# A bidirectional delta-rule scan: four of eight operators evicted by two engines, and the order of the stage and of the end laid out anew

## The chip, the cores and the metric

The kernel runs on one core of a Trainium2 chip. The metric is the device time of one launch, in microseconds; lower is better. PE (TensorE) multiplies and PEld loads its weights; DVE (VectorE), ACT (ScalarE) and POOL (GpSimd) are the element-wise engines; SP (SyncE) issues DMAs. Each engine runs its instructions in one fixed order, and an instruction at the front of its queue that waits holds everything behind it on that engine.

## The reference

One layer of a sequence model on 128 context tokens and 2048 latent tokens of width 1024, in float32:

```python
h    = rmsnorm(x, norm_g) * (1 + scale) + shift
r, k, v, g_a, b_gate, c_gate, u_conv, g_b = split(h @ w_in)
r, k, v = token_shift(r, k, v)
# head group A, 8 heads x 64, in two directions: the delta rule
def step(S, inp):
    r_t, w_t, k_t, v_t, kk_t, a_t = inp
    s_kk = einsum('bdhij,bdhj->bdhi', S, kk_t)
    S = (S * w_t[..., None, :] - s_kk[..., :, None] * (kk_t * a_t)[..., None, :]
         + v_t[..., :, None] * k_t[..., None, :])
    return S, einsum('bdhij,bdhj->bdhi', S, r_t)
ya = (groupnorm(sum of both directions) + bonus) * silu(g_a)
# head group B: a gated convolution of three taps
yb = b_gate * conv3(c_gate * u_conv) * silu(g_b)
out = rmsnorm(x + gate * (concat(ya, yb) @ w_out), final_g)
```

The outputs are the context and latent tokens and the final states S of the context.

## The kernel before

The launch has three parts. **Part 1** makes the modulation, the norm, the input projection (each float32 factor as a high and a low fp32r part, three products), the token shift, the gates and the convolution; it writes the scan's operands to DRAM. Its first products for the scan are begun early. **Part 2** is the scan, and **part 3** the output projection with its residual and last norm.

*The scan.* It is chunked: 64 tokens of a head pair are a unit. A stage is 8 units of one head pair in one direction and 8 in the other (its two groups, gi 0 and 1). There are 16 latent stages and one for the context (stage 15; the last one, 16, is latent), 17 in all. Within a unit the delta rule becomes matrix products, and between units a state of 64x64 per head is carried. A stage is written in words; the last digit is the group, and a digit ahead of it numbers halves or units:

- Gm, Qm, Fm: products of the operands on PE (L1019, L1028). Ge, Fe: their masks on DVE (L1037). Fa, Qe: copies on ACT (L1051, L1048).
- dg, ab, zi, pre: the diagonal blocks, turned and prepared (DVE L1058, L1063, L1081, L1082, ACT L1073 to L1075). I: the inverse of 32x32 triangles for both groups, 45 instructions on POOL in 15 steps of one L1091 and two L1094, each from the step before it.
- zr, zd (DVE L1102, L1105), c0, c1 (ACT L1111), U, bu, W, n (PE L1119, ACT L1122, PE L1127, ACT L1130): the inverse of the 64x64 triangles from those of the 32x32 ones. gh: operand copies on ACT (L1160, L1161).
- X, Xc: the solve on PE (L1171) and its eviction on ACT (L1175).
- E: eight operators a stage (16 matmuls each, L1189) into a PSUM tile of 128x512. Ev: the mask that evicts such a tile, on DVE (L1194), all 512 columns; of each 128 columns the first 64 meet ones in the mask.
- S, sv: one step of the state on PE (L1220: an operator times state and values, state and outputs at once) and the scaling of the new state on DVE (L1246). y: the outputs of four units, copied by ACT (L1267) or added by DVE (L1265). POOL clears the first state of the context (L1215) and copies a held state (L1213).
- fw, fr, fq, fm, T, fy, fa: the group norm and gate of a finished block of 512 tokens (L1298 to L1323), written to DRAM in mixT.

*What sets the order.* `SEQ` lists the words of one body; `word+d` does the word for the stage d later, so body b has the states of stage b, the operators of b and b+1, the inversion of b+2 and the products of b+3. Bodies 0 to 12 are this list again and again; from there on `LATE` lists every word with its stage (`word@stage`), and the words of part 3 among them. The orders of PE, DVE and ACT are those of the lists. POOL and SP are not under the lists; the framework places their instructions by what they depend on.

*PSUM.* Three pools lie beside each other: four buffers for the states and T, U, W, two "s" buffers, and two "m" buffers. `IN_PM` names the products that take "m"; the others, and E from stage 14 and X from stage 15 on, take "s".

*Words of part 3.* R closes the "m" pool and opens part 3. CL, CH, CD and WL, WH, WD load w_out's convolution and attention rows and split them in two (load L1468, high on ACT, low on DVE or POOL). AL, AH, AD and aL, aH, aD do that for the tokens of a tile (L1483, L1490). AP and AE are the convolution products of tiles 5, 6 and 7, done ahead, and their eviction (L1503 to L1505). P, B: convolution and attention products; Z, G, Q, ss, rt, rc, fo: gate, residual (POOL L1568) and norm.

Of the kernel before, what the change touches and what calls it, by code (L numbers as in the profile page):

```python
# [10 lines left out]
ALU = mybir.AluOpType  # L11
# [746 lines left out]
fsL0+1 gsL0+2 sv01 fr Ev100 Gm1+3 Ge1+3 dg1+3 W+1 S11 Qm1+3 gh11+1 gh00+1 ab+3 fq Fm0+3 S30 n+1 Qe1+3 Qm0+3  # L758
L0+4 sv11 Fa0+3 Qe0+3 zi+3 sv30 S40 Fe0+3 fm S21 sv40 sv21 Fm1+3 L1+4 X0+1 S50 pre+3 T sv50 Fa1+3 Fe1+3 S31
S60 sv31 Xc00+1 init+1 y00 Xc10+1 X1+1 S41 Xc01+1 sv60 S70 svL0+2 zr+2 sv41 E000+1 sv70 fy Xc11+1 Ev000+1  # L760
zd+2 S51 gh01+2 U+2 y01 Gm0+4 E001+1 c0+2
"""
IN_PM = "E001 E011 E101 E110 Fm1 Gm1 Qm0 Qm1 X1".split()
IN_S = "T U W".split()
FIXED = 13
LATE = """
I@15 sv51@12 fa@10.1 Ge0@16 E110@13 Ev001@13 gh10@14 E010@13 Ev110@13 E100@13 gh00@14 Ev010@13 Gm1@16
fsL0@14 Ev100@13 gh11@14 S00@13 Ge1@16 S61@12 E111@13 c1@14 sv00@13 E011@13 sv61@12 bu@14 dg0@16 S10@13
Ev011@13 S71@12 E101@13 svL1@14 fw@11.0 sv10@13 sv71@12 y10@12 S20@13 fsL1@14 Ev111@13 S01@13 y11@12 W@14
sv20@13 sv01@13 Ev101@13 S30@13 n@14 S11@13 sv30@13 sv11@13 S40@13 fr@11.0 X0@14 sv40@13 fq@11.0 dg1@16  # L770
X1@14 fm@11.0 Xc00@14 ab@16 S50@13 S21@13 Xc10@14 T@11.0 Xc01@14 E000@14 sv50@13 sv21@13 S60@13 Ev000@14
# [10 lines left out]
Ev000@15 fq@14.0 E011@15 fm@14.0 W@16 fsL1@16 gsL1@16 gh01@16 Ev001@15 WD@1 CL@7 Ev011@15 E010@15 gh11@16
T@14.0 fsL0@16 gsL0@16 gh10@16 S00@15 CL@6 fy@14.0 S30@15 S20@15 S01@15 gh00@16 S11@15 fa@14.0 S31@15 S21@15
sv30@15 n@16 Ev010@15 sv00@15 sv20@15 fw@14.1 X1@16 CH@7 fr@14.1 S10@15 S40@15 S60@15 Xc01@16 CD@7 S70@15
Xc11@16 sv40@15 WL@3 sv11@15 sv01@15 sv21@15 sv10@15 CH@6 X0@16 S50@15 CD@6 Xc00@16 S41@15 S61@15 S51@15
sv51@15 Xc10@16 WL@2 sv50@15 sv41@15 sv70@15 sv31@15 fq@14.1 E110@16 fm@14.1 E000@16 sv60@15 WH@3 sv61@15
S71@15 Ev110@16 sv71@15 E111@16 WD@3 Ev000@16 E001@16 Ev111@16 E101@16 Ev001@16 WH@2 AL@5 E100@16 y10@15
WD@2 Ev100@16 y00@15 T@14.1 E010@16 fy@14.1 S00@16 fa@14.1 S01@16 Ev010@16 AH@5 E011@16 AD@5 AL@6 Lo@0 xL@5
sv00@16 AP0@5 y01@15 y11@15 aL@5 fc@15.1 AP1@5 AE0@5 Ev101@16 fw@15.1 fr@15.1 xL@6 sv01@16 Ev011@16 AH@6
S10@16 S11@16 AE1@5 AD@6 aH@5 sv10@16 AP0@6 AL@7 fq@15.1 aD@5 fm@15.1 aL@6 sv11@16 AP1@6 AE0@6 P0l@5 B0@5  # L790
AH@7 AE1@6 AD@7 aH@6 cL@8 aD@6 aL@7 AP0@7 Z0@5 G0@5 AP1@7 AE0@7 P1l@5 B1@5 AE1@7 cH@8 cD@8 cL@9 P0l@6 B0@6
aH@7 Q0@5 aD@7 Z1@5 aL@8 P1r@6 B1@6 Z0@6 G1@5 xL@7 G0@6 P0r@7 B0@7 Z1@6 aH@8 Q0@6 aD@8 G1@6 Q1@5 aL@9 P1l@7
B1@7 ss@5 Q1@6 xL@8 ss@6 S20@16 P0l@8 sv20@16 aH@9 rt@5 aD@9 rt@6 rc@5 aL@10 fo@5 B0@8 rc@6 fo@6 S30@16
P1r@8 sv30@16 y00@16 Z0@7 Z1@7 G0@7 cH@9 S40@16 B1@8 sv40@16 G1@7 cD@9 Z0@8 cL@10 xL@9 G0@8 aH@10 S50@16
P0r@9 sv50@16 Q0@7 aD@10 Z1@8 Q0@8 aL@11 Q1@7 G1@8 ss@7 S60@16 rt@7 T@15.1 sv60@16 Q1@8 xL@10 S70@16 B0@9
sv70@16 fy@15.1 fa@15.1 y10@16 ss@8 fw@16.0 P1l@9 fr@16.0 rc@7 fq@16.0 fm@16.0 fo@7 B1@9 cH@10 cD@10 cL@11
P0l@10 aH@11 rt@8 aD@11 rc@8 aL@12 fo@8 B0@10 Z0@9 Z1@9 G0@9 G1@9 Q0@9 P1r@10 Z0@10 xL@11 G0@10 cH@11 T@16.0
Q0@10 cD@11 B1@10 fy@16.0 cL@12 fa@16.0 P0r@11 aH@12 Q1@9 aD@12 Z1@10 aL@0 ss@9 G1@10 rt@9 B0@11 rc@9 fo@9
# [12 lines left out]
G0@3 Q0@3 B1@3 cH@4 cD@4 P0r@4 Z1@3 G1@3 Q1@3 B0@4 ss@3 rt@3 rc@3 fo@3 P1l@4 Z0@4 G0@4 Q0@4 B1@4 Z1@4 G1@4
Q1@4 ss@4 rt@4 rc@4 fo@4
"""


def phase2(K):
    nc, tc, A, S = K.nc, K.tc, K.A, K.S
    V, G, P, T = nc.vector, nc.gpsimd, nc.scalar, nc.tensor
    D = nc.sync.dma_start
    MF, MG, ME = (0, 1), (0, 1), (2, 3)  # L820
    B = Ctx()
# [151 lines left out]
    def stage(s):  # L973

        if s in sts:
            return sts[s]
        st = sts[s] = Ctx()
        st.g = []
        st.fin = None
        for d, units, blk in stages[s]:  # L980
            g = Ctx()
            g.d, g.units, g.blk = d, units, blk
            g.E, g.ps, g.sp = {}, {}, {}
            st.g.append(g)
        return st

# [190 lines left out]
    def operator(name, s, st, gi):  # L1177

        g = st.g[gi]
        n, h2 = (int(c) for c in name[-3:-1])  # L1180
        us = half(g, n)
        k = (h2 if g.d == 0 else 1 - h2) * 2
        if name[:2] != "Ev":
            lt, rt = (g.fs, g.gs) if g.d == 0 else (g.gs, g.fs)
            pe = g.ps[name] = psum(name, s, [128, 2, 2, 128])
            for i in range(2):
                for hd in range(2):
                    for b, r in enumerate((H0, H1)):
                        T.matmul(pe[r, i, hd, :].rearrange("p (b t) -> p b t", b=2), lt[:, b, hd, us.start + k + i], rt[:, :, hd, us.start + k + i], start=True, stop=True)  # L1189
# [4 lines left out]
        V.tensor_tensor(g.E[n][:, k:k + 2].rearrange("p a b c -> p (a b) c"), pe[:].rearrange("p a b c -> p (a b) c"),  # L1194
                        B.msk[:, ME[g.d]].unsqueeze(1).broadcast_to((128, 4, 128)), ALU.mult)
# [137 lines left out]
    def ending(name, s, st, gi):  # L1333
# [3 lines left out]
        if st.fin is not None:  # L1337
# [311 lines left out]
```

## Time and profile before

| | us |
|---|---|
| median of 3 runs (1585.86 to 1587.49) | 1586.96 |
| the profiled execution, by the same clock as the runs | 1585.76 |
| its span in the profile | 1583.9 |
| steady scan, inversions 2 to 15 | 964.4 to 1307.5 |
| end of inversion 16 | 1337.7 |
| U of stage 16 begins | 1341.5 |
| first convolution product of part 3 begins | 1375.5 |

The profile is one execution, 1.86 us outside the span. In a group's row stand the line, the engine, the operation, output and inputs with partitions x elements, the count, then busy us and mean ns of one, then idle time of the engine just ahead of them and what ended most of it. In a timeline row stand the start, the length, and in brackets an idle time before it and its end's cause; a count x32 is a run of such instructions. A row of waits holds the waiting engine and line, what it waited for, the total us, the times and the longest. In windows, each engine's busy us stands with its number of instructions.

### The profile page before, as it was taken

Reading aid. Unit: us, or ns where it says so; the run is one execution under the profiler, and the core shown is the slowest. Engines: PE = TensorE matmul, PEld = TensorE weight load, DVE = VectorE, ACT = ScalarE, POOL = GpSimd, SP = SyncE. Lnnn points to the kernel's source line nnn. Section 1 sums busy time; section 2 is a strip of 40 time slices with the busy share of each in tenths; the row PEclk is TensorE's granted clock in tenths of the full one; section 3 lists DMA queues with packets and bytes.
Section 4 is the critical chain, followed back from the end, with each engine's and each line's share of the span. In section 5 each row is a group of like instructions: output and inputs, shape, how many; then the busy total and the mean of one; then the engine's idle time right before and its main releaser. Section 6 shows DMA issues by size and latency. Waiting matters only on the chain.

```text
span 1583.9 us, 39394 instructions
## 1 busy us (share of the span) xinstructions
PE 1501.7 (95%) x16208; PEld 1382.2 (87%) x16208; DVE 1137.6 (72%) x1960; ACT 770.6 (49%) x1460; POOL 570.9 (36%) x961
## 2 busy tenths in 40 slices
PE   5899999999999999999999998999999887899998
PEld 2799999999999999899999997888888776778786
DVE  5889996673999735349985438899898977746533
ACT  4466652432555213225551117887778767523221
POOL 0033331000333100013322705888888885212221
PEclk8899999999999999999999998999999999999999
DMA  9569999663878865447897537567576754645442
GB/s 371 197 168 269 269 268 335 216 222 112 218 231 227 203 230 181 145 137 209 262 242 271 184 125 193 151 177 195 167 205 167 186 149 149 186 134 188 147 144 93
DMA packets 204580, 313.78 MB, mean 198 GB/s; under 512 B 58089, under 2 KB 147561, under 8 KB 190321
## 3 DMA queue, kind: packets, MB, share of 16 engines
q1 hardware_dynamic: 168816, 311.13, 63.3%
q10 hardware_dynamic: 35584, 0.14, 1.4%
q8 instruction: 127, 2.08, 0.6%
q14 instruction: 53, 0.43, 0.1%
HBM read 208.05 MB, written 103.17 MB: 196 GB/s over the span
## 4 chain that ended last, share of the span: by engine, by line
PE 57%; POOL 18%; DVE 10%; issue 7%; DMA 5%; ACT 3%; SPq 1%; ACTq 0%; DVEq 0%; POOLq 0%
POOL zt L1094 11%; POOL ztmp L1091 7%; PE psu L1503 4%; PE psu L1505 4%; PE psu L1504 4%; PE mmb L182 2%; PE mmb L184 2%; PE mmb L183 2%; PE mmc L182 2%; PE mmc L184 2%; PE mmc L183 2%; PE mmu L184 2%; PE mmu L182 2%; PE mmgb L183 2%; PE mmgb L182 2%
## 5 line engine op out<-in xcount | busy, mean ns | idle before, releaser
L1094 POOL TENSOR_TENSOR zt<-zt,ztmp 128x30 f32<-128x30 f32 (+7 forms) x510 | 217.5, 426 | 39.8
L1091 POOL TENSOR_TENSOR ztmp<-ab,zt 128x60 f32<-128x60 f32 (+7 forms) x255 | 137.7, 540 | 65.3 <-DVE ab L1082 45.6
L410 POOL TENSOR_TENSOR sh<-rawl 128x384 f32<-128x384 f32 (+1 forms) x48 | 47.1, 997 | 210.4 <-ACT rawl L401 210.4
L1220 PEld LDWEIGHTS psS<-sv,E 128*64 128x64 f32 x2176 | 81.5, 137 | 40.7 <-DVE sv L1246 18.7
L1220 PE MATMUL psS<-sv,E 128*64 128x64 f32 x2176 | 102.4, 228 | 15.1 <-DVE sv L1246 10.4
L1194 DVE TENSOR_TENSOR E<-psE,msk 128x512 f32<-128x512 f32 x136 | 90.6, 682 | 20.7 <-PE psE L1189 19.8
L1568 POOL TENSOR_TENSOR z<-z,x 128x512 f32<-128x512 f32 x32 | 42.7, 1337 | 148.9 <-DVE z L1562 86.2
L1175 ACT ACTIVATE stf<-psX 64x512 f32<-64x512 f32 x136 | 80.3, 591 | 10.6 <-PE psX L1171 8.1
L434 POOL TENSOR_TENSOR hsl<-sq,hsh 128x384 fp32r<-128x384 f32 (+1 forms) x24 | 32.5, 1356 | 141.9 <-ACT hsh L429 141.9
L1246 DVE TENSOR_TENSOR sv<-psS,pc 64x128 f32<-64x128 f32 x254 | 62.3, 271 | 20.0 <-PE psS L1220 19.4
L182 PE MATMUL mmg<-h,w 128*128 128x384 f32 (+1 forms) x216 | 70.9, 328 | 0.0
L183 PE MATMUL mmg<-h,w 128*128 128x384 f32 (+1 forms) x216 | 70.8, 328 | 0.0
L184 PE MATMUL mmg<-h,w 128*128 128x384 f32 (+1 forms) x216 | 70.7, 327 | 0.0
L219 POOL TENSOR_TENSOR hslq<-ssq,hshq 128x384 fp32r<-128x384 f32 (+1 forms) x4 | 4.8, 1207 | 174.8 <-ACT hshq L218 110.3
L182 PE MATMUL mmv<-h,w 128*128 128x384 f32 (+1 forms) x192 | 63.9, 333 | 3.7 <-ACT lf L665 3.1
L182 PE MATMUL mmb<-h,w 128*128 128x384 f32 (+1 forms) x192 | 63.6, 331 | 3.8 <-DMA w<-scr_wsp 3.8
L184 PE MATMUL mmb<-h,w 128*128 128x384 f32 (+1 forms) x192 | 63.6, 331 | 0.0
L183 PE MATMUL mmb<-h,w 128*128 128x384 f32 (+1 forms) x192 | 63.3, 330 | 0.0
L184 PE MATMUL mmv<-h,w 128*128 128x384 f32 (+1 forms) x192 | 63.3, 330 | 0.0
L183 PE MATMUL mmv<-h,w 128*128 128x384 f32 (+1 forms) x192 | 63.2, 329 | 0.0
L182 PE MATMUL mmc<-h,w 128*128 128x384 f32 (+1 forms) x192 | 63.1, 329 | 0.0
L184 PE MATMUL mmc<-h,w 128*128 128x384 f32 (+1 forms) x192 | 62.9, 327 | 0.1
(311 smaller groups left out, 5018.2 us busy)
## 6 DMA issues: line engine op xcount, KB each, us to landing
w<-scr_wsp SPq DMA_DIRECT2D x68, 1024.0 KB, 6.5
scr_wsp<-w SPq DMA_DIRECT2D x34, 1024.0 KB, 6.4
rr<-scr_ops SPq DMA_DIRECT2D x32, 1024.0 KB, 6.4
scr_ops<-xs SPq DMA_DIRECT2D x160, 192.0 KB, 6.5
wr<-in_win SPq DMA_DIRECT2D x34, 512.0 KB, 6.6
x<-in_x SPq DMA_DIRECT2D x17, 512.0 KB, 3.8
wadas<-in_wada SPq DMA_DIRECT2D x8, 1024.0 KB, 13.9
sv<-scr_vt SPq DMA_DIRECT2D x32, 256.0 KB, 4.0
```

Source lines behind the costliest of these rows:

```text
L182: T.matmul(ps[:, :n], w[:, 0, k], hh[:, 0, k, :n], start=k == 0, stop=False)
L183: T.matmul(ps[:, :n], w[:, 0, k], hh[:, 1, k, :n], start=False, stop=False)
L184: T.matmul(ps[:, :n], w[:, 1, k], hh[:, 0, k, :n], start=False, stop=k == 7)
L1091: G.tensor_tensor(tv, ab[:, j:j + 2, j + 2:32].unsqueeze(1).broadcast_to((128, kn, 2, n)), zt[:, :kn, j:j + 2].unsqueeze(3).broadcast_to(( ...
L1094: G.tensor_tensor(zt[:, :kn, j + 2:32], zt[:, :kn, j + 2:32], tv[:, :, r], ALU.subtract)
L1175: P.activation(g.fs[64:128, :, hd, e::2], g.ps["X"][e][hr_].rearrange("p a (b t) -> p b a t", b=2), AF.Copy, scale=-1.0)
L1194: V.tensor_tensor(g.E[n][:, k:k + 2].rearrange("p a b c -> p (a b) c"), pe[:].rearrange("p a b c -> p (a b) c"), B.msk[:, ME[g.d]].unsquee ...
L1220: T.matmul(g.sp[i // 4][r, q, hd, :], g.E[n][:, k, hd, r], g.sv[:, u, hd, :], start=True, stop=True)
L1246: V.tensor_tensor(dst, g.sp[i // 4][0:64, q], B.pc[0:64, d, 2 * p:2 * p + 2, c:c + 1].broadcast_to((64, 2, 64)), ALU.mult)
L1503: T.matmul(ps[:], mh[:, n], hi[:, cs], start=start and n == 0, stop=False)
L1504: T.matmul(ps[:], mh[:, n], lo[:, cs], start=False, stop=False)
L1505: T.matmul(ps[:], ml[:, n], hi[:, cs], start=False, stop=stop and n == 3)
```

## The change

A new word, Ea, does the first half of four of the eight operators: ACT copies columns 0 to 63 of each 128 without a mask, and DVE masks columns 64 to 127. The four are E000, E001, E100 and E101. The half mask waits for the copy. All words of the two lists change places, and Fm0 and Gm0 take the "m" buffers instead of E001, E101, E110, Qm0 and Qm1.

```diff
 SEQ = """
-S00 sv51+-1 fa+-1 S61+-1 Ge0+3 dg0+3 gh10+1 sv61+-1 E110 sv00 S71+-1 svL1+1 y10+-1 Ev001 S10 c1+1 Ev110 sv10
-E111 sv71+-1 Ev111 E010 E101 y11+-1 E011 gsL1+2 fsL1+1 bu+1 Ev010 I+2 S20 Ev101 fw Ev011 sv20 S01 E100
...
+S00 fa+-1 y01+-1 sv61+-1 sv00 E100 gh01 E001 Ge0+3 c1+1 Ea001 S71+-1 svL1+1 Ea100 S10 sv71+-1 Ev001 y11+-1
+y10+-1 I+2 sv10 fw Ev100 E011 S01 sv01 dg0+3 Ev011 E101 Ea101 fr c0+1 S20 Qm1+3 S11 Gm1+3 gh10+1 Ev101 sv11
...
-IN_PM = "E001 E011 E101 E110 Fm1 Gm1 Qm0 Qm1 X1".split()
+IN_PM = "E011 Fm0 Fm1 Gm0 Gm1 X1".split()
...
 LATE = """
...
-E010@14 zi@16 Xc11@14 sv60@13 S31@13 Ev010@14 S70@13 E100@14 svL0@15 sv70@13 sv31@13 pre@16 I@16 E110@14 Ev100@14
...
-S71@14 CH@4 E110@15 svL1@16 sv71@14 E100@15 CH@5 CD@4 fw@14.0 CD@5 WL@0 zr@16 WL@1 zd@16 U@16 fr@14.0 c1@16
-y11@14 c0@16 Ev100@15 Ev110@15 E111@15 bu@16 E101@15 Ev111@15 WH@0 E000@15 Ev101@15 WH@1 E001@15 WD@0
...
-S10@16 S11@16 AE1@5 AD@6 aH@5 sv10@16 AP0@6 AL@7 fq@15.1 aD@5 fm@15.1 aL@6 sv11@16 AP1@6 AE0@6 P0l@5 B0@5
...
+fr@11.1 Qm0@16 pre@16 fq@11.1 Fa0@16 Qe1@16 Qe0@16 sv71@12 fm@11.1 bu@14 I@16 sv00@13 Fe0@16 S10@13 y11@12
...
+zr@16 S20@14 Xc10@15 sv20@14 zd@16 fw@14.1 X1@15 fr@14.1 S30@14 Xc01@15 U@16 sv30@14 y00@14 Xc11@15 CH@7
+E100@15 E000@15 fq@14.1 CD@7 WH@0 S40@14 fm@14.1 Ea000@15 WL@1 WD@0 c0@16 sv40@14 T@14.1 Ev000@15 c1@16
+fy@14.1 E001@15 fa@14.1 S50@14 AL@5 S00@15 Ea001@15 sv50@14 bu@16 Ev001@15 sv00@15 E111@15 S60@14 Ev111@15
...
+E100@16 fc@15.1 Ea001@16 WD@2 AP0@6 Ea100@16 AE1@5 Ev001@16 Ev100@16 WH@3 AL@7 E111@16 AE0@6 WD@3 fw@15.1
...
-        if name[:2] != "Ev":
+        if name[1].isdigit():
             lt, rt = (g.fs, g.gs) if g.d == 0 else (g.gs, g.fs)
...
-        pe = g.ps.pop("E" + name[-3:])
-        V.tensor_tensor(g.E[n][:, k:k + 2].rearrange("p a b c -> p (a b) c"), pe[:].rearrange("p a b c -> p (a b) c"),
-                        B.msk[:, ME[g.d]].unsqueeze(1).broadcast_to((128, 4, 128)), ALU.mult)
+        dst, pe = (x.rearrange("p a b c -> p (a b) c") for x in (g.E[n][:, k:k + 2], g.ps["E" + name[-3:]][:]))
+        if name[:2] == "Ea":
+            P.copy(dst[:, :, 0:64], pe[:, :, 0:64])
+            g.plain.add(name[-3:])
+            return
+        c0 = 64 if name[-3:] in g.plain else 0
+        V.tensor_tensor(dst[:, :, c0:], pe[:, :, c0:], B.msk[:, ME[g.d], c0:].unsqueeze(1).broadcast_to((128, 4, 128 - c0)), ALU.mult)
+        g.ps.pop("E" + name[-3:])
```

In the rows below a line number of the changed kernel is one to six higher than that of the same instruction before (L1091 is L1092, L1194 is L1200, L1246 is L1252).

First DVE in a steady body, the body of stage 9, before: the masks (L1194) with the scaled states (L1246) between them. psE001_9 is the PSUM tile of operator E001 of stage 9.

```order
L1246 TENSOR_TENSOR sv_1409_13651<-psS9_0_0_14226,pc_9573 64x128
L1194 TENSOR_TENSOR E01_1464_14262<-psE001_9_1460_14215,msk_8349 128x512
L1194 TENSOR_TENSOR E10_1465_14270<-psE110_9_1462_14245,msk_8349 128x512
L1246 TENSOR_TENSOR sv_1409_13651<-psS9_0_0_14226,pc_9573 64x128
L1246 TENSOR_TENSOR sv_1420_13774<-psS8_1_4_14122,pc_9573 64x128
L1194 TENSOR_TENSOR E11_1467_14283<-psE111_9_1466_14273,msk_8349 128x512
```

The same place on DVE now, and then on ACT.

```order
L1252 TENSOR_TENSOR sv_1420_13782<-psS8_1_4_14164,pc_9573 64x128
L1200 TENSOR_TENSOR E01_1462_14265<-psE001_9_1461_14252,msk_8349 128x4x64
L1252 TENSOR_TENSOR sv_1412_13699<-psS9_0_0_14230,pc_9573 64x128
L1200 TENSOR_TENSOR E10_1464_14273<-psE100_9_1460_14241,msk_8349 128x4x64
L1252 TENSOR_TENSOR sv_1420_13782<-psS9_1_0_14344,pc_9573 64x128
```

```order
L1161 COPY sth1_9589<-GA01_8369 64x8x64
L1162 COPY sth1_9589<-Q01_8370 64x8x64
L1112 COPY zb_9594<-zd_1452_14162 32x16x32 x2
L1196 COPY E01_1462_14265<-psE001_9_1461_14252 128x4x64
L1196 COPY E10_1464_14273<-psE100_9_1460_14241 128x4x64
```

The masks of E001 and E100 are 256 elements instead of 512, and two copies of ACT on the same PSUM tiles stand behind the copies of gh and c.

Then POOL where inversion 15 ends and inversion 16 begins, before: zt_1609 belongs to stage 15, zt_1657 to stage 16, and the cleared sv to the context stage.

```order
L1091 TENSOR_TENSOR ztmp_1629_16180<-ab_1605_15930,zt_1609_15968 128x60
L1094 TENSOR_TENSOR zt_1609_15968<-zt_1609_15968,ztmp_1629_16180 128x15x2 x2
L1215 MEMSET sv_1659_16536 64x128 x4
L1091 TENSOR_TENSOR ztmp_1660_16543<-ab_1652_16466,zt_1657_16511 128x60
L1094 TENSOR_TENSOR zt_1657_16511<-zt_1657_16511,ztmp_1660_16543 128x30 x2
```

The same place now (zt_1609 belongs to stage 15, zt_1648 to stage 16).

```order
L1092 TENSOR_TENSOR ztmp_1627_16200<-ab_1603_15931,zt_1609_16015 128x60
L1095 TENSOR_TENSOR zt_1609_16015<-zt_1609_16015,ztmp_1627_16200 128x15x2 x2
L1092 TENSOR_TENSOR ztmp_1652_16453<-ab_1643_16368,zt_1648_16428 128x60
L1095 TENSOR_TENSOR zt_1648_16428<-zt_1648_16428,ztmp_1652_16453 128x30 x2
```

The clears have left this place; both stand behind the last step of inversion 16.

Last, PE around U of stage 16 and the operators of stage 15, before.

```order
L1189 MATMUL psE110_15_1693_17009<-stg0_9582,stf0_9576 64x128 x8
L1189 MATMUL psE100_15_1696_17022<-stg0_9582,stf0_9576 64x128 x8
L1119 MATMUL psU_16_1701_17046<-zr_1699_17040,GA10_8372 32x32 x16
L1119 MATMUL psU_16_1701_17046<-zr_1699_17040,GA11_8375 32x32 x16
L1189 MATMUL psE111_15_1704_17089<-stf1_9577,stg1_9583 64x128 x8
L1189 MATMUL psE101_15_1705_17100<-stf1_9577,stg1_9583 64x128 x8
L1189 MATMUL psE000_15_1707_17114<-stg0_9582,stf0_9576 64x128 x8
```

And now.

```order
L1120 MATMUL psU_16_1698_17066<-zr_1691_17025,GA11_8375 32x32 x16
L1190 MATMUL psE100_15_1699_17104<-stg0_9582,stf0_9576 64x128 x8
L1190 MATMUL psE000_15_1700_17113<-stg0_9582,stf0_9576 64x128 x8
L1226 MATMUL psS14_0_4_17127<-sv_1622_16156,E10_1680_16829 64x64 x4
L1323 MATMUL psT_0_1703_17144<-idt2_8359,y_1660_16603 128x2x64 x4
L1190 MATMUL psE001_15_1704_17153<-stf1_9577,stg1_9583 64x128 x8
L1226 MATMUL psS14_0_4_17127<-sv_1622_16156,E10_1680_16829 64x64 x4
L1226 MATMUL psS15_0_0_17171<-sv_1671_16761,E00_1702_17136 64x64 x4
L1190 MATMUL psE111_15_1706_17183<-stf1_9577,stg1_9583 64x128 x8
```

U now stands ahead of all operators of stage 15, whose rows alternate with states of stages 14 and 15. The mask that frees E100's PSUM buffer stands on DVE behind the masks of E000, E001, E111 and E011.

More of the change, by code (lines that the diff above doesn't have):

```diff
@@ L766 @@
 LATE = """
[L767 to L771, printed above, removed]
@@ L782 @@
[L782 to L786, printed above, removed]
@@ L982, in stage @@
             g.d, g.units, g.blk = d, units, blk
-            g.E, g.ps, g.sp = {}, {}, {}
+            g.E, g.ps, g.sp, g.plain = {}, {}, {}, set()
             st.g.append(g)
@@ L1341, in phase2 @@
               zr=zrows, zd=zrows, c0=zcopies, c1=zcopies, U=merge, bu=merge, W=merge, n=merge, gh=gcopies, X=solve, Xc=solve,
-              E=operator, Ev=operator, S=state, sv=scaled, y=outputs,
+              E=operator, Ev=operator, Ea=operator, S=state, sv=scaled, y=outputs,
               fw=ending, fr=ending, fq=ending, fm=ending, T=ending, fy=ending, fa=ending)
```

82 lines of the change are left out of this document (46 added, 36 removed).

## The prediction

> **What bounds the kernel now.** I read the page first: busy shares, then the chain that ended last.
>
> ```profile
> span 1583.9 us, 39394 instructions
> PE 1501.7 (95%) x16208; PEld 1382.2 (87%) x16208; DVE 1137.6 (72%) x1960; ACT 770.6 (49%) x1460; POOL 570.9 (36%) x961
> PE 57%; POOL 18%; DVE 10%; issue 7%; DMA 5%; ACT 3%; SPq 1%; ACTq 0%; DVEq 0%; POOLq 0%
> ```
>
> POOL is busy for a third of the span only, yet 18% of the chain runs through it. So there is a stretch in which POOL is the bound, and the change lies in that stretch. I therefore cut the scan and what follows into windows. The columns are length, then busy time of PE, PEld, DVE, ACT and POOL, granted clock, DMA share, GB/s. The first two rows are two single stages, the others the whole steady scan, the two stretches behind it, and the output products.
>
> ```profile
> 1135.20:1159.90 24.70, 23.07 (x592) 19.98 (x590) 23.78 (x48) 18.26 (x36) 21.22 (x45) 1.00 0.68 193
> 1184.40:1209.30 24.90, 23.23 (x600) 20.50 (x597) 21.57 (x44) 20.99 (x41) 21.44 (x45) 1.00 0.63 187
> 964.30:1307.50 343.20, 319.53 (x8167) 281.03 (x8161) 299.78 (x603) 267.32 (x507) 293.84 (x630) 0.99 0.63 175
> 1307.50:1341.50 34.00, 27.07 (x628) 23.13 (x626) 26.05 (x56) 25.85 (x47) 22.72 (x56) 1.00 0.48 139
> 1341.50:1375.50 34.00, 28.42 (x569) 24.35 (x569) 24.35 (x47) 23.04 (x36) 9.38 (x4) 0.90 0.59 173
> 1375.50:1583.90 208.40, 198.56 (x942) 158.71 (x940) 99.75 (x168) 53.69 (x130) 42.81 (x33) 0.98 0.45 147
> ...
> L1094 POOL TENSOR_TENSOR zt<-zt,ztmp 128x56 f32<-128x56 f32 (+7 forms) x415 | 178.9, 431 | 32.5
> L1091 POOL TENSOR_TENSOR ztmp<-ab,zt 128x192 f32<-128x192 f32 (+7 forms) x207 | 112.6, 544 | 16.2
> ```
>
> By plain busy time PE and DVE look like the bound (319.5 and 299.8 of 343.2). But the last two rows are POOL's groups between 966 and 1306, and their idle time names no releaser: 48.7 us over 622 instructions is 78 ns behind each, the same after every one, and the list of POOL's waits for this stretch is empty. POOL runs 14 inversions back to back: 343.2 / 14 = **24.5 us a stage**. A stage gets shorter only if an inversion does; it gets longer only if the input of the next inversion comes late. Behind the scan PE is busy for 198.6 of 208.4 us: that part is PE's.
>
> **The masks.** These are the rows for the two half jobs, with one wait of DVE on POOL, and DVE's wait for E:
>
> ```profile
> L1194 DVE TENSOR_TENSOR E<-psE,msk 128x512 f32<-128x512 f32 x112 | 74.4, 682 | 13.6 <-PE psE L1189 12.8
> L1037 DVE TENSOR_TENSOR F<-psFm,msk 128x256 f32<-128x256 f32 x53 | 19.6, 408 | 0.0
> L1051 ACT COPY F<-psFm 128x256 f32<-128x256 f32 x52 | 16.9, 376 | 7.3 <-PE psFm L1019 7.3
> ...
> DVE zr L1102 <- POOL zt L1094: 9.5, 9, 1.7
> DVE E L1194 <- PE psE L1189: 12.8, 34, 3.4
> ```
>
> Half a mask has the shape of L1037, 0.41 us instead of 0.68; the copy has the shape of L1051, 0.38 us. With four operators a stage, DVE loses 4 x 0.27 = 1.1 us and ACT gains 4 x 0.38 = 1.5. ACT's busiest stage above goes from 21.0 to 22.5 of 24.9 us, DVE's from 23.8 to 22.7. Both stay under POOL's 24.5, so **the steady scan gets 0**; POOL hides it. If POOL did not bound, the 1.1 us of DVE would be worth up to 14 x 1.1 = 15 us.
>
> The change also adds a wait. Each half mask waits for the copy of its own operator, so the two stand in series: 0.38 + 0.41 = 0.79 us, where one mask took 0.68, and the copy stands behind other ACT work (a gh or c pair, two copies of 0.61 us). Behind the waiting mask on DVE stand the scaled states (sv) and the next mask, and PE waits for both, for the PSUM buffer and for the state. That is not in the trace of before. Below: nothing, if PE delivers early enough. Above: 4 x (1.2 + 0.38) = 6.3 us a stage, if DVE had nothing to do meanwhile. The nearest row is DVE's wait for E, 12.8 / 34 = 0.38 us each, so I take 4 x 0.38 = 1.5 us a stage. DVE has 9.5 / 14 = 0.7 us of waiting for POOL and the saved 1.1, together 1.8. 1.5 fits in, just. So 0 stands, with an open upper side.
>
> **Does a lighter DVE speed up POOL?** One inversion step is stretched in this piece of the timeline, and another is not:
>
> ```profile
> 974.76 0.63 POOL L1091 TENSOR_TENSOR ztmp<-ab,zt 128x256 f32<-128x256 f32 x1
> 973.98 1.27 DVE L1194 TENSOR_TENSOR E<-psE,msk 128x512 f32<-128x512 f32 x2
> ...
> 985.91 1.34 POOL L1091 TENSOR_TENSOR ztmp<-ab,zt 128x60 f32<-128x60 f32 x1
> 985.95 1.11 DVE L1081 TENSOR_TENSOR dg<-ab 128x512 f32<-128x512 f32 x1
> 1306.52 0.31 POOL L1091 TENSOR_TENSOR ztmp<-ab,zt 128x60 f32<-128x60 f32 x1
> ```
>
> The 60-element step takes 0.31 us alone and 1.34 beside L1081, whose inputs both lie in SBUF. Beside two E masks, which read PSUM, the 256-element step takes 0.63, about its mean. So removing E columns from DVE gives POOL 0.
>
> The Trainium skill, "GPSIMD Engine Reference", section Specifications, says that GpSimd shares its SBUF interfaces with VectorE and contends only with instructions in a 2-port mode or with two SBUF inputs. That speaks against a gain in the scan, and the two pairs of rows agree with it; if any DVE work counted, 1.1 us less of it a stage could give up to 15 us.
>
> **The end lists.** After stage 14's words the order is new. The rows are POOL's around the last two inversions, DVE's last input to the last one, and PE's first product that needs it:
>
> ```profile
> 1306.91 0.61 POOL L1094 TENSOR_TENSOR zt<-zt,ztmp 128x30 f32<-128x30 f32 x2
> 1311.04 0.63 POOL L1215 MEMSET sv<- 64x128 f32 x4 [3.52 <-PE psS L1220]
> 1313.61 0.28 POOL L1091 TENSOR_TENSOR ztmp<-ab,zt 128x60 f32<-128x60 f32 x1 [1.94 <-DVE ab L1082]
> 1337.11 0.60 POOL L1094 TENSOR_TENSOR zt<-zt,ztmp 128x30 f32<-128x30 f32 x2
> ...
> 1312.77 0.69 DVE L1082 TENSOR_TENSOR ab<-ab,dg 128x512 f32<-128x512 f32 x1
> ...
> 1341.46 1.61 PE L1119 MATMUL psU<-zr,GA 32*32 32x32 f32 x64 [1.99 <-DVE zr L1102]
> ```
>
> Inversion 15 ends at 1307.5, inversion 16 starts at 1313.6: POOL clears a state buffer, and DVE's L1082 comes late. In the new order DVE does L1082 for stage 16 among the words of body 13, and both clears stand behind inversion 16. It can follow at once, **6.1 us earlier**, and end near 1331.6 (1337.7 − 6.1); then U of stage 16 is not late. The clears hold nothing there: the first state of stage 15 stands on PE behind that U. PE, however, runs in order with the same work (a mask or copy is none of PE's), so the end gains only what PE idles or runs at half clock:
>
> ```profile
> 1287.30:1294.20 6.90, 4.76 (x63) 4.37 (x64) 2.24 (x4) 6.77 (x12) 5.96 (x13) 0.51 0.27 81
> 1342.00:1348.80 6.80, 5.65 (x86) 5.51 (x82) 4.08 (x7) 5.81 (x9) 1.75 (x1) 0.50 0.41 144
> 1393.20:1396.60 3.40, 3.40 (x9) 2.56 (x9) 2.10 (x4) 0.39 (x1) 0.87 (x1) 0.51 0.39 114
> ...
> 1289.44 0.42 PE L1119 MATMUL psU<-zr,GA 32*32 32x32 f32 x7 [2.42 <-issue]
> 1392.64 0.50 PE L1503 MATMUL psa<-woh,mhc 128*128 128x512 f32 x1 [2.14 <-ACT mhc L1490]
> 1374.43 1.09 PE L1189 MATMUL psE<-stf,stg 128*64 128x128 f32 x16 [0.43 <-DVE E L1194]
> ...
> 1382.42 9.45 DMA mxc<-scr_mixT
> ...
> PE psX L1171 <- ACT stf L1175: 1.4, 2, 0.8
> PE psX L1171 <- ACT zb L1130: 0.8, 2, 0.6
> PE psE L1189 <- DVE E L1194: 2.4, 4, 1.2
> ```
>
> Each of three PE gaps (2.42, 1.99, 2.14 us) is followed by a stretch at a granted clock of about a half. In it half of PE's busy time is lost: 2.4, 2.8 and 1.7 us.
> - U of stage 16: −2.0 idle, −2.8 clock.
> - X of stage 16 waits for ACT (1.4 + 0.8, between 1341.5 and 1375.5). In the new list the state words of stage 15 stand between: −2.2.
> - The third conv product (AP of tile 7) waits for a late load and its rounding. The load's piece of the chain is 9.45 us long. The new list issues it ahead of six operators of stage 16 (1.09 us of PE each by the row at 1374.43), and of AP1 of tile 6, and on SP's queue ahead of the gate, gain and x loads, behind which it stands today; 6.5 us and that product lie between, about the load's length, so its wait goes: −2.1 idle, −1.7 clock.
> - One operator of stage 15 (E100) keeps one of the two PSUM buffers until after the fifth, so five share the other. Such waits are 1.2 us at the longest today, 2.4 together; I double them: **+2.4**, with 0 and five of the longest less today's, 5 x 1.2 − 2.4 = 3.6, as bounds.
> - A gap there may drop the clock anew: between 0 and 2.8, I take 2.4, the drop at 1287.
>
> The first gap, a wait for issue, stays. The sum is −4.8 − 2.2 − 3.8 + 2.4 + 2.4 = **−6.0 us**. It agrees with POOL's 6.1 us, by another way.
>
> The Trainium skill, "TensorE: Matmul & The Clock Gate", Part 1: The HAM clock gate, has the clock fall back only after an idle window of about 3.4 us. By that rule gaps of 2 us cost no clock; the three clock terms (−2.8, −1.7, +2.4) would be struck, and the sum would be −3.9. The three rows disagree with the rule, and they decide.
>
> The profiled execution took 1585.76 us (span 1583.9), the median is 1586.96; applied to the median the forecast is **1581.0 us**.
>
> **The rivals.** *The new wait binds (slower).* The stage becomes DVE's as soon as the half masks wait for more than 1.8 us a stage in all. From there each further 0.5 us costs 14 x 0.5 = 7 us. At 1.0 us it is 1586.96 − 6 + 14 = 1595. For it: up to 6.3 us by the bound, and DVE's stage of 23.8 us has little air. Against: POOL's input need only arrive in time, and DVE waits only for what its other work does not cover.
>
> *The end gives back its gain (no change).* PE's work behind 1307.5 is unchanged, and 208.4 us of it are 95% busy. If the buffer costs 3.6 and a new drop 2.8, and the late load stays, −4.8 − 2.2 + 6.4 = −0.6: 1586.4.
>
> *A light DVE speeds POOL, or the change isn't what it says.* The first would give up to 15 us, 1581 − 15 = 1566; the rows exclude nearly all of it. The second: the copy runs ahead of the mask, in series, not beside it; that is the slower rival, already priced.
>
> **The numbers.** Two runs 0.2% apart (3.2 us) are about what a measurement of this kernel can tell. Forecast with an end gain of over 3.2 us: 0.52; more than that, by a faster POOL: 0.03; no change: 0.24; slower: 0.21. The terms' bounds give −6 with both added costs at nothing, −10.8, to −0.6: 1576 to 1586. If the first gap goes too (2.4 idle, 2.4 clock) it is 1571; that is unlikely, and the range starts at 1572. With the slower rival at half a microsecond a stage over its point it is 1588, and at 0.8 it is 1592, where the range ends; 0.08 is left out below and 0.12 above.
>
> **What would show it.** POOL without a wait between 964 and the end of inversion 16, and 24.5 us each; inversion 16 right behind 15; U of stage 16 without a wait, 6 us earlier; L1196 at 0.38 and the half L1200 at 0.41; the half-clock stretches behind U and before the third conv product gone; an output part of about 208 us. Wrong is the forecast if POOL waits for L1083 in the steady scan: then the slower rival holds, and DVE's waits for L1196 name it. It is also wrong if PE idles more around the operators of stage 15 than the 12.5 us (6.9 + 5.6) of the two stretches behind 1307.5.

## The result, and the profile after

The changed kernel takes **1604.64 us** (median of 4 runs, 1602.52 to 1611.63), the kernel before 1586.41 beside it: ratio 1.0124, 95% interval 1.0096 to 1.0152. It is slower by some 18 us; the forecast was 1581.0 with a range to 1592. (Left out of the time and ratio of x11 below are two of its launches, at a granted clock of 0.69 and 0.75 instead of some 0.98, and one of the kernel before that took 3670 us.) The profiled execution is the slowest of the four (1611.63 us), and its page shows another chain:

```profile
span 1609.8 us, 39530 instructions
PE 1517.8 (94%) x16208; PEld 1398.0 (87%) x16208; DVE 1123.7 (70%) x1960; ACT 792.9 (49%) x1528; POOL 560.4 (35%) x961
PE 69%; DVE 15%; DMA 6%; issue 6%; ACT 3%; SPq 1%; ACTq 0%; POOL 0%; DVEq 0%; POOLq 0%
...
L1200 DVE TENSOR_TENSOR E<-psE,msk 128x512 f32<-128x512 f32 (+1 forms) x136 | 74.1, 548 | 31.4 <-ACT E L1196 16.6
```

DVE's masks did get cheaper (74.1 us instead of 90.6), and POOL has left the chain that ended last (0% instead of 18%). POOL is no longer the bound; somebody keeps it waiting. The waits between 966 and 1306: POOL's only one (the list of before is empty there), DVE's for the new copies, PE's of the kind "issue", and the same of before:

```profile
POOL ztmp L1092 <- DVE ab L1083: 51.4, 10, 15.2
...
DVE E L1200 <- ACT E L1196: 12.5, 15, 2.9
...
PE psE L1190 <- issue: 7.4, 4, 2.6
PE psS L1226 <- issue: 6.3, 3, 2.6
PE psGm L1020 <- issue: 6.0, 3, 2.4
PE psX L1172 <- issue: 1.5, 2, 1.0
...
PE psE L1189 <- issue: 3.3, 5, 1.1
PE psU L1119 <- issue: 2.9, 2, 2.4
```

POOL waits for the input of its inversion; 15.2 of the 51.4 us are the entry into the scan, as before (14.5, just ahead of 966). The rest is new. PE in turn stands still for 21 us in which it waits for nothing that the profile shows ("issue"). In the same stretch of before there were 6.2 us of this (2.9 at U, 3.3 at E), 2.4 of them once.

The starts of the inversions in POOL's timeline cut each profile into parts (us; gaps: PE's issue gaps over 1 us between 966 and 1335, number and sum):

```
                start 2  2 to 3  3 to 15  15 to end   gaps
before            964.4    24.0    295.4      300.1   3,  5.0
changed           966.9    29.6    313.2      300.1  12, 24.0
x1 no rr          969.8    32.1    292.7      293.3   0
x2 no copy        964.2    27.9    310.0      301.3  11, 19.5
x4 spread         963.5    27.6    304.5      300.0   8, 14.8
x6 rr behind      964.2    28.0    315.1      295.3   0
x8 split alone    969.8    28.7    297.3      299.4   4,  5.7
x9 Qm0 late       966.5    27.8    296.9      293.6   0
x10 stores        961.7    24.0    308.4      300.4  12, 18.2
x11 end alone     964.2    24.1    296.3      295.2   2,  2.2
x12 rr last       964.9    28.4    295.2      298.3   2,  3.9
```

Each row is one execution; that of the changed kernel is 7 us above its median. The changed kernel's 25.9 us of span are thus 2.5 ahead of inversion 2, 5.6 in the first stage, 17.8 in the twelve steady ones and 0 in the end. Ten of its gaps, with 20.5 us, lie in the twelve steady stages, and two in the end. Before, x8 and x10 each have one gap of 1.45 us, right behind the start of inversion 16, that is of another kind than the rest (next paragraphs).

**What the gaps are.** One stage of the changed kernel: SP's timeline, then PE's around a gap, then the windows ahead of the gap and behind it (columns as in the prediction), then two pieces of the DMA view, for 1198.2 to 1207.2 and for 1207.2 to 1208.8 (queue, kind: packets, MB, share of the 16 engines).

```profile
1198.03 0.37 SPq L1010 DMA_DIRECT2D rr<-scr_ops  x1
1199.01 0.58 SPq L957 DMA_DIRECT2D stg<-scr_ops  x1
1199.64 2.09 SPq L957 DMA_DIRECT2D stf<-scr_ops  x2
1201.78 0.60 SPq L957 DMA_DIRECT2D stg<-scr_ops  x1
1202.83 0.38 SPq L1010 DMA_DIRECT2D rr<-scr_ops  x1
...
1206.58 0.93 PE L1190 MATMUL psE<-sth,stf 128*64 128x128 f32 x13
1210.07 0.33 PE L1190 MATMUL psE<-sth,stf 128*64 128x128 f32 x2 [2.56 <-issue]
...
1202.00:1207.50 5.50, 5.35 (x145) 4.48 (x137) 5.02 (x12) 4.89 (x10) 2.95 (x10) 1.00 1.09 243
1211.10:1214.50 3.40, 3.40 (x53) 3.13 (x49) 2.26 (x6) 2.02 (x4) 2.93 (x7) 0.50 0.29 87
...
q1 hardware_dynamic: 1101, 2.11, 93.5%
...
q1 hardware_dynamic: 222, 0.44, 98.4%
q8 instruction: 1, 0.02, 5.2%
```

The page has 127 packets of kind "instruction" on queue q8 with 2.08 MB: 16 KB each, or one for about 255 of PE's 32416 matmuls and weight loads. From 1198.0 to 1207.3 none begins; the DMA engines are full (share 1.09 from 1202 on) with 3 MB of operands. The next one begins at 1207.3, PE stops at 1207.5, in the middle of one operator's 16 matmuls, and runs again at 1210.07. Behind the gap the granted clock is 0.50 for 3.4 us.

The other eleven gaps are like it. Each ends 2.6 to 2.9 us after such a packet began. And if PE's records in the trace (matmuls, weight loads and its sequencer's, 32706 in all) are counted from the first one, every one of the twelve gaps begins behind the 193rd or 194th record of a block of 256. PE stops where the instructions of one packet end and those of the next have not come. Both gaps of x12 and eleven of x10's twelve stand at such places too; the gap of 1.45 us in before doesn't (159th), and it is not one of a late packet.

Before, the same loads stand like this (a stage between 1170 and 1181):

```profile
1170.81 0.58 SPq L956 DMA_DIRECT2D stg<-scr_ops  x1
1171.44 1.76 SPq L956 DMA_DIRECT2D stf<-scr_ops  x2
1173.25 0.60 SPq L956 DMA_DIRECT2D stg<-scr_ops  x1
1173.95 0.54 SPq L1286 DMA_DIRECT2D w<-scr_q  x1
1177.75 2.71 SPq L1009 DMA_DIRECT2D rr<-scr_ops  x2
```

Four small loads, a pause of 4 us with one other load of 256 KB in it, then both large ones. In the changed kernel one large load comes first, and the four small ones and the second large one follow without a pause: each load waits for the last word that reads its tile, and these words have changed places.

### The profile page after: what moved, and what is told of

It reads as the page before. It is cut to its first block, busy times and chain, and to the rows that moved or that the text cites. A ratio compares the mean times of both kernels' runs of the same rounds, so it can differ in the third digit from the quotient of the medians.

```text
span 1609.8 us, 39530 instructions
## 1 busy us (share of the span) xinstructions
PE 1517.8 (94%) x16208; PEld 1398.0 (87%) x16208; DVE 1123.7 (70%) x1960; ACT 792.9 (49%) x1528; POOL 560.4 (35%) x961
## 3 DMA queue, kind: packets, MB, share of 16 engines
q8 instruction: 127, 2.08, 0.5%
## 4 chain that ended last, share of the span: by engine, by line
PE 69%; DVE 15%; DMA 6%; issue 6%; ACT 3%; SPq 1%; ACTq 0%; POOL 0%; DVEq 0%; POOLq 0%
PE psE L1190 7%; PE psS L1226 4%; PE psu L1509 4%; PE psu L1511 4%; PE psu L1510 4%; PE psGm L1020 2%; DMA stf<-scr_ops 2%; PE psFm L1020 2%; PE mmb L184 2%; PE mmb L183 2%; PE mmb L182 2%; PE mmu L182 2%; PE mmu L184 2%; PE mmu L183 2%; PE mmc L182 2%
## 5 line engine op out<-in xcount | busy, mean ns | idle before, releaser
L1095 POOL TENSOR_TENSOR zt<-zt,ztmp 128x30 f32<-128x30 f32 (+7 forms) x510 | 206.3, 405 | 40.0
L1092 POOL TENSOR_TENSOR ztmp<-ab,zt 128x60 f32<-128x60 f32 (+7 forms) x255 | 135.7, 532 | 102.3 <-DVE ab L1083 83.4
L1226 PE MATMUL psS<-sv,E 128*64 128x64 f32 x2176 | 107.7, 232 | 19.3 <-DVE sv L1252 11.1
L1226 PEld LDWEIGHTS psS<-sv,E 128*64 128x64 f32 x2176 | 89.4, 142 | 40.8 <-issue 22.1
L1252 DVE TENSOR_TENSOR sv<-psS,pc 64x128 f32<-64x128 f32 x254 | 64.9, 275 | 57.5 <-PE psS L1226 56.3
L1200 DVE TENSOR_TENSOR E<-psE,msk 128x512 f32<-128x512 f32 (+1 forms) x136 | 74.1, 548 | 31.4 <-ACT E L1196 16.6
L182 PE MATMUL mmb<-h,w 128*128 128x384 f32 (+1 forms) x192 | 62.8, 327 | 3.9 <-DMA w<-scr_wsp 3.9
L182 PE MATMUL mmu<-h,w 128*128 128x384 f32 (+1 forms) x192 | 62.8, 327 | 0.3 <-DMA w<-scr_wsp 0.3
L184 PE MATMUL mmu<-h,w 128*128 128x384 f32 (+1 forms) x192 | 62.8, 327 | 0.0
```

Source lines behind the costliest of these rows:

```text
L182: T.matmul(ps[:, :n], w[:, 0, k], hh[:, 0, k, :n], start=k == 0, stop=False)
L184: T.matmul(ps[:, :n], w[:, 1, k], hh[:, 0, k, :n], start=False, stop=k == 7)
L1092: G.tensor_tensor(tv, ab[:, j:j + 2, j + 2:32].unsqueeze(1).broadcast_to((128, kn, 2, n)), zt[:, :kn, j:j + 2].unsqueeze(3).broadcast_to(( ...
L1095: G.tensor_tensor(zt[:, :kn, j + 2:32], zt[:, :kn, j + 2:32], tv[:, :, r], ALU.subtract)
L1200: V.tensor_tensor(dst[:, :, c0:], pe[:, :, c0:], B.msk[:, ME[g.d], c0:].unsqueeze(1).broadcast_to((128, 4, 128 - c0)), ALU.mult)
L1226: T.matmul(g.sp[i // 4][r, q, hd, :], g.E[n][:, k, hd, r], g.sv[:, u, hd, :], start=True, stop=True)
```

## The experiments

Theory 1: PE's instruction fetch comes late behind the operand loads. Theory 2: the half masks' wait for the copies. Theory 3: the order of the compute words or the PSUM buffers. Ratios are to the kernel before on the same chip.

**x1, without the rr loads from stage 4 on** (the changed kernel; later results are not the reference's):

```diff
+        if s == 4:
+            V.memset(g.rr[:, 0:4], 0.0)
+        if s < 4:
             ...
```

> The changed kernel without the operand loads (rr) from stage 4 on; their tile is set to zero once instead, so the scan's later results are not the reference's and 2 MB a stage are not moved. Theory 1 (the rewritten list bunches a stage's loads; PE's own instruction fetch comes late behind them; PE stands still for some 2.4 us and runs at half clock after it): the issue gaps of PE over 1 us in the scan fall from some ten to at most two, and the time from 1604 to 1578 to 1590. Theory 2 (the half mask waits for ACT's copy, and DVE and PE with it): nothing of that changes, 1600 to 1606. Theory 3 (the order of the compute words and the PSUM buffers): also 1600 to 1606.

1587.29 us, ratio 1.0014 (0.9993 to 1.0036), and no issue gap. Theory 1 held. The first stage is 2.5 us longer than the changed kernel's; the clearing of the tile (two DVE instructions of 1.76 us) is among it.

**x2, the lists without the split operators:**

```diff
-            P.copy(dst[:, :, 0:64], pe[:, :, 0:64])
-            g.plain.add(name[-3:])
             return
```

> The changed kernel with both new lists, but the word Ea does nothing and DVE masks all 512 columns of every operator. Theory 2: the wait is gone, the time falls by 10 us or more, to 1585 to 1595. Theory 1: the issue gaps stay at eight or more, and the time stays at 1600 to 1610 (1.1 us a stage more on DVE hides behind them).

1605.07 us, ratio 1.0121 (1.0086 to 1.0156), eleven gaps: the new wait is not what costs. Theory 2 fell.

**x3, x4 and x5 did not do what they were meant to.** x3 (kernel before) and x4 (changed) move load words in the list:

```diff
-... gsL1+2 fsL1+1 ... fsL0+1 gsL0+2 ... L0+4 ...
+... L0+4 gsL0+2 fsL0+1 fsL1+1 gsL1+2 ...
```

> The kernel before, with the words of four loads a stage (gs and fs of both groups) moved to right behind the first rr load, so that 3 MB come in one burst; no compute word moves. Theory 1: five or more issue gaps of PE over 1 us in the scan instead of two, each with a half-clock stretch, and 1593 to 1610. Theories 2 and 3: 1585 to 1589, or a little more if the operators wait for the loads themselves, which the waits would name.

> The changed kernel with the two rr load words of a body put later (behind X0 and behind S31), some 3 us and more after the four fs and gs loads; no compute word moves. Theory 1: issue gaps over 1 us at most four, 1578 to 1594. Theories 2 and 3: 1600 to 1606. If the loads come too late instead, PE waits for rr at the next products, and the waits name that DMA.

SP's timelines show the loads where they were, in x3 four small ones and then two large ones behind a pause, in x4 a large, four small and a large one: SP's order is the framework's, and the place of a load word doesn't set it. So neither tests a theory. x3 measured 1583.23 us, ratio 0.9991 (0.9970 to 1.0013); x4 1597.95, ratio 1.0078 (1.0051 to 1.0105), with eight gaps instead of twelve. By the traces every engine of x4 does the changed kernel's instructions in the changed kernel's order, and of the loads one alone (of the context, at 1269 us) has another place. So x4 is in effect the changed kernel measured a second time, and eight gaps against twelve, 0.0078 against 0.0124, is how far two such measurements lie apart. x5 adds a DRAM to DRAM transfer of 1 MB a stage to the kernel before:

```diff
         load_stk(g.fs, g, 2)
+        if gi == 1 and 3 <= s < 15:
+            D(S["dum"][s], S["ops0"][0, 0:128, 0:2048])
```

> The kernel before with one added transfer of 1 MB a stage (stages 3 to 14), DRAM to DRAM, issued right behind the four gs and fs loads and read by nobody; no compute word moves. Theory 1 (PE's instruction fetch late behind saturated DMA engines): the pause between these loads and the rr loads is filled, five or more issue gaps of PE over 1 us in the scan, 1595 to 1615. Theory 3 (the order of the compute words): no such gaps, 1585 to 1590.

1628.17 us, ratio 1.0269 (1.0238 to 1.0299), but the transfers wait for nothing and were all issued ahead of the scan (738.8 to 770.2): inversion 2 starts 41 us later, and the stages are as before. It says nothing of the scan.

**x6, E110 and E111 ahead of Fm0** (changed kernel):

```diff
-Fm0+3 L0+4 E110 gsL0+2 fsL0+1 gh00+1 Ev110 bu+1 W+1
-Qe0+3 Fa0+3 Fe0+3 zi+3 n+1 sv30 E111 fsL1+1 gsL1+2 Ev111 gh11+2 T Fm1+3 L1+4
+E110 gsL0+2 fsL0+1 gh00+1 Ev110 E111 fsL1+1 gsL1+2 bu+1 W+1
+Qe0+3 Ev111 zi+3 n+1 sv30 Fm0+3 L0+4 gh11+2 T Fa0+3 Fe0+3 Fm1+3 L1+4
```

> The changed kernel with one move in the body's list: the operators E110 and E111 come ahead of the product Fm0, so that the four gs and fs loads, which wait for these operators, are issued ahead of both rr loads and not between them. Theory 1: issue gaps over 1 us at most four, 1578 to 1594. Theory 3 in its other forms (PSUM buffers, the half masks): 1600 to 1606.

1608.68 us, ratio 1.0146 (1.0129 to 1.0163): no gap, as theory 1 had it, but not its 1578 to 1594. A new wait of PE has taken the gaps' place, Fm1 for the buffers that Fm0's mask frees, 1.8 us a stage.

```profile
PE psFm L1020 <- DVE F L1038: 23.4, 13, 2.3
```

**x9, only the product Qm0 later** (changed kernel). Qm0 is the last reader of the first rr tile:

```diff
-fq U+1 Qm0+3 Qe1+3 ... Fm0+3 L0+4 E110 ... Qe0+3 Fa0+3 ... sv30 E111 fsL1+1 gsL1+2 Ev111 gh11+2
+fq U+1 Qe1+3 ... Fm0+3 E110 ... Fa0+3 ... sv30 E111 fsL1+1 gsL1+2 Qm0+3 L0+4 Ev111 Qe0+3 gh11+2
```

> The changed kernel with one product of the body, Qm0 (and its copy Qe0), put behind the operator E111. It is the last reader of the first rr tile, so the first rr load now follows the four gs and fs loads, as in x6, but Fm0 keeps its place and Fm1 its buffers. Theory 1: no issue gap of PE over 1 us with DMA engines saturated ahead of it, at most four in the scan, stages of 24.3 to 25.0 us between inversions 3 and 15, 1578 to 1592. If a new wait takes the place of the gaps, as in x6, the waits of PE name it, and the stages stay at 26.

1584.99 us, ratio 1.0013 (0.9997 to 1.0030), no gap, and 24.7 us a stage (296.9 / 12).

**x12, the load order alone** (changed kernel). A one-column ACT instruction reads the first rr tile and an operator that is finished late, so the load must wait; PE and DVE keep their order:

```diff
+        if name == "gh11" and 3 <= s < 14:
+            P.activation(B.tick[:], B.rr.tiles[0][:, 0, 0, 0:1], AF.Identity, bias=sts[s - 2].g[1].E[1][:, 0, 0, 0:1], scale=1.0)
...
-Fm0+3 L0+4 E110 ... Ev111 gh11+2
+Fm0+3 E110 ... Ev111 gh11+2 L0+4
```

> The changed kernel, in which one ACT instruction of 128x1 a stage (from stage 3 on) reads a finished operator and the first rr tile, so that the first rr load is issued behind the four gs and fs loads instead of ahead of them. The order of PE and DVE is that of the changed kernel, instruction by instruction. Theory 1 in its narrow form (the order of the loads alone makes PE's instruction fetch late enough to stop PE): at most four issue gaps of PE over 1 us in the scan, and 1580 to 1592, as x9. If x9 was fast because of the moved product Qm0: eight or more gaps and 1598 to 1606.

1590.25 us, ratio 1.0027 (1.0010 to 1.0045), two gaps instead of twelve (x4: eight), 24.6 us a stage. SP's timeline of one stage, and PE's largest wait in the scan:

```profile
1185.60 0.58 SPq L958 DMA_DIRECT2D stg<-scr_ops  x1
1186.23 2.10 SPq L958 DMA_DIRECT2D stf<-scr_ops  x2
1188.38 0.60 SPq L958 DMA_DIRECT2D stg<-scr_ops  x1
1189.44 0.93 SPq L1011 DMA_DIRECT2D rr<-scr_ops  x2
...
PE psGm L1021 <- DMA rr<-scr_ops: 11.4, 11, 1.6
```

The same 3 MB without a pause, but with the large loads last, cost 1.0 us a stage at Gm0, which the slack of a stage takes, in place of the gaps. The changed kernel is 0.0124 over the kernel before (1.0096 to 1.0152), by x4 0.0078 (1.0051 to 1.0105), and both intervals lie above that of x12. The order of these loads is thus worth about 0.010 by the one and 0.005 by the other.

**x10, more traffic in the kernel before:**

```diff
+        if name == "Ev100" and 1 <= s < 13:
+            for m in range(2):
+                D(S["dum"][s, :, m * 1024:m * 1024 + 1024], g.E[m][:].rearrange("p a b c -> p (a b c)"))
```

> The kernel before with two added stores of 512 KB a stage in stages 1 to 12 (finished operators to a DRAM tensor that nobody reads), issued when the mask of E100 is done, that is around the four gs and fs loads and ahead of the rr loads; no compute word moves. Theory 1: the pause between the loads is filled, five or more issue gaps of PE over 1 us in the scan, 1592 to 1610. Against it: no more than two such gaps, 1584 to 1590; waits for the stores themselves, if any, show as waits of DVE on a DMA.

1595.07 us, ratio 1.0105 (1.0050 to 1.0160), twelve gaps, eleven of them where a packet's instructions end, and the order of every compute word is that of before. No wait of DVE on a DMA appears. SP's timeline of a stage, and PE's waits in the scan:

```profile
1102.10 0.32 SPq L1198 DMA_DIRECT2D scr_dum<-E  x1
1103.12 0.59 SPq L956 DMA_DIRECT2D sth<-scr_ops  x1
1103.76 1.28 SPq L956 DMA_DIRECT2D stf<-scr_ops  x2
1105.09 0.60 SPq L956 DMA_DIRECT2D sth<-scr_ops  x1
1105.74 0.58 SPq L1198 DMA_DIRECT2D scr_dum<-E  x1
...
1109.58 3.15 SPq L1009 DMA_DIRECT2D rr<-scr_ops  x2
...
PE psS L1223 <- issue: 7.2, 5, 1.9
PE psU L1119 <- issue: 4.6, 4, 2.0
```

Loads removed or put in another order end the gaps (x1, x9, x12), traffic added brings them (x10). That is theory 1 from both sides. Theory 3 falls with it as far as the gaps go: in x12 PE, DVE and POOL keep the changed kernel's order, and in x10 that of before.

**x8, the split operators alone** (kernel before, Ea right behind its product in the body's list, as E100 Ea100):

> The kernel before with the split operators alone: Ea right behind the products of E001, E000, E100 and E101 in the body's list, and no other word moved. Theory 1: POOL stays the bound at 24.5 us a stage, 1584 to 1589. Theory 2 (the half mask's wait for the copy): 1592 or more, with POOL's waits for L1083 in the steady scan.

1589.65 us, ratio 1.0039 (1.0019 to 1.0059), just above theory 1's range and below theory 2's. Steady stages of 24.8 us; 4.7 us are lost in the first one, where one mask waits 8.0 us for its copy:

```profile
DVE E L1199 <- ACT E L1195: 19.1, 16, 8.0
```

**x7 and x11, the end.** x7 moves dg1, ab, zi, pre and I of stage 16 right behind dg0 in the old end list; x11 keeps the old list for bodies 0 to 12 and takes the new end list whole, with the words ahead that the two lists share out differently:

```diff
 LATE = """
+sv51@12 S61@12 Ge0@16 gh11@14 Ea001@13 Ev001@13 E010@13 Ev010@13
 I@15 gh01@13 ...
```

> The kernel before with five words of the end list put earlier (dg1, ab, zi, pre, I of stage 16, behind dg0): the inversion of stage 16 follows that of stage 15 without a pause, and nothing else of the change is done. The prediction's sum: the wait of U of stage 16 (2.0) and its half-clock stretch (2.8) go, 1579 to 1584. Its rival (the end gives the gain back): 1585 to 1588.

> The bodies 0 to 12 with the list of before (no split operator in them), and from there on the end list of the changed kernel with its split operators and its PSUM buffers; seven words that the two lists share out differently stand at the head of the end list. The prediction's sum for the end: inversion 16 right behind 15, and from the start of inversion 15 to the end of the span some 294 us instead of 300.1, as x1 (293.3) and x9 (293.6) have it; stages 2 to 15 as before; 1577 to 1583. Its rival (the end gives the gain back, as in the changed kernel with 300.1): 1584 to 1588.

x7: 1591.54 us, ratio 1.0049 (1.0031 to 1.0067), slower, which neither forecast had. Inversion 16 follows at once (1311.3), but U of stage 16 still waits 1.99 us for zr at 1344.6, because zr and U keep their late places, and PE has a new wait of 4.2 for a scaled state, since DVE stands at the five words:

```profile
PE psS L1219 <- DVE sv L1245: 6.6, 7, 4.2
PE psE L1188 <- DVE E L1193: 4.6, 5, 2.1
```

x11: 1583.86 us, ratio 1.0005 (0.9992 to 1.0017): no change. Its profiled execution has 295.2 us from inversion 15 to the end.

## Why the prediction was wrong

- **The bound.** Right: POOL at 24.5 us a stage sets the scan as soon as nothing else is late (x9 and x11: 24.7, and POOL has no wait between inversions 3 and 15; x12, at 24.6, still has 6.6 us of waits there).
- **The masks, 0 in the steady scan.** Right, and the mechanism too: without the copies the kernel is as slow (x2), and the split alone adds about 0.2 us a stage (297.3 against 295.4 in twelve). The half masks take 0.41 us and the copies 0.37. They do wait for the copies, 12.5 us in the scan, 5.0 of them in the first stage; that leaves 0.6 a stage (7.5 / 12), where 1.5 was taken. The rival "the new wait binds" would have given a time as high as the measured one, but by a mechanism that x2 excludes. The prediction's sign for it, POOL waiting for L1083, did come (36 us) and had another cause. The 4.7 us of the first stage in x8 were not foreseen.
- **The step that failed** is "so the steady scan gets 0; POOL hides it". It moved compute words and priced the compute. Each of these words is also the last reader of a tile that the next load fills; the list of moved steps had no line for the rr, gs and fs loads, the bulk of the scan's traffic. Moved, they bring ten gaps of PE with 20.5 us into the twelve steady stages, and a half-clock stretch behind five of them; 17.8 us of that are more than the slack takes.
- **"The same work" for PE** is true and misled: the same instructions have to be fetched, and their packets come late when the DMA engines are full of operands.
- **No port relief.** Nothing contradicts it: with the lighter DVE and no gaps (x9) a stage is still 24.7 us.
- **The end, −6.0.** In the changed kernel 0. Inversion 16 does start right behind 15 (24.6 us after its start), U of stage 16 no longer waits for zr, and the third conv product no longer for its load, as forecast; the buffer's +2.4 came out at +0.7 (PE waits 3.1 us for E's masks instead of 2.4). What failed here is the clock. The sum has −2.8 − 1.7 + 2.4 = −2.1 for it, with 2.8 as the most that a new drop costs. With the new end list a stretch of 13.7 us at 0.50 (10.2 in x6) stands around U of stage 16. In x11 PE is busy for 12.5 us of it and, reckoned as in the prediction, loses half of that, 6.3:

```profile
1335.40:1349.10 13.70, 12.53 (x184) 10.25 (x184) 9.72 (x13) 8.73 (x15) 4.65 (x6) 0.50 0.70 192
...
PE psS L1227 <- DVE sv L1253: 6.3, 12, 3.0
```

Ahead of it stand short waits of PE for scaled states, in x11 five of 0.15 to 0.50 us in 6 us. The longest wait for one, 3.0 us at 1302, has 6.8 us of half clock behind it, another 3.2 lost. From the start of inversion 15 to the end of the span PE is idle for 24.9 to 27.9 us and loses 5.0 to 8.1 to the half clock with the old end list (before, x3, x5, x8, x10), and 20.1 to 24.2 and 7.5 to 10.7 with the new one (the changed kernel, x1, x2, x4, x6, x9, x11, x12). x11 against x5, neither of which stops for a packet there: idle −4.0, and the sum's idle terms make −2.0 − 2.2 − 2.1 + 2.4 = −3.9; clock +4.5 instead of −2.1. So the end is 295.2 us against 296.3, the time saved in waits is mostly paid back in clock, and x11's timed runs exclude a gain of more than 1.3 us (0.0008 x 1583). In the changed kernel two gaps (1.3 and 2.2 us) come on top; the 300.1 of before holds a gap of 2.4 with its half clock at 1289, which x5 hasn't. Why the clock falls behind waits so short stays open.
- **Half clock after gaps of about 2 us.** Borne out: in the changed kernel six of the eight gaps of 2.1 to 2.6 us are followed by 3.4 us at 0.50 (those that end at 1232.9 and 1267.7 are not). The Trainium skill, "TensorE: Matmul & The Clock Gate", Part 1: The HAM clock gate, puts the limit at idle windows of some 3.4 us; the rows differ, and they decide. But such gaps are not the only way to a half clock, as the 13.7 us of the end show.
- The sum of the change by the ratios: the loads' order 0.005 to 0.010 (x12 against x4 and the changed kernel); the rest, 0.0027, is about what the first stage costs more (4 us of 1586 in x12). That stage takes 27.6 to 28.4 us with the new list in x4, x6, x9 and x12, and 27.9 without the copies (x2), so the lists alone cost it nearly 4 us.

No version of the change beats the kernel before: x9 and x11 come out even with it.

## What to carry to other kernels

A word that is moved takes along the DMA that waits for it: draw up when each load is issued before and after, and how long the DMA engines are full without a pause. Where an engine runs through hundreds of instructions in a few microseconds, its own instruction packets are one more user of these engines, and a gap marked "issue" in the middle of a run of like instructions is the sign. An order list for three engines isn't an order list for the fourth; look at SP's timeline before taking a moved load for moved. And where many short waits take the place of one long one, look at the granted clock behind them before booking the gain.

## What the runs showed of the hardware

PE's instruction packets (16 KB, for some 255 instructions) came 3.4 to 7.2 us apart in the changed kernel where the DMA share between them was under 0.5 (1000 to 1335 us), and up to 9.4 us apart behind 3 MB of operand loads. The twelve packets that PE stopped for came 5.8 to 9.4 us after the one before, and PE stood still for 1.0 to 2.6 us. Counted in the blocks of 256 from above, PE began a packet's instructions in no run sooner than 2.18 us after the packet had begun (some 65 packets a run, between 966 and 1335 us).

Not every late packet stops PE for long: between 970 and 1306 us x9 has six intervals over 7.3 us and x6 ten, without a gap over 1 us, and x12 seven with two. All three have waits of PE of their own at that place (x9: 13.7 us for scaled states in the scan; x6: 23.4 for Fm1's buffers; x12: 11.4 for rr); that these gave the packet its time was only argued.
